# RMSNorm and Swish: transfers of 3, 5 and eight times 15 rows, computed in units of five rows

## The chip, the cores and the metric

The kernel runs on one core of a Trainium2 chip. The metric is the device time of one execution in microseconds (us); each number quoted is the median of several executions. The profile's span is about 2 us shorter than that time.

Engine names as in the profile: DVE is VectorE, ACT is ScalarE, POOL is GpSimd, SP is SyncE. ACTq and SPq are the sequencers of ACT and SP, which issue transfers. DMA stands for the core's 16 transfer engines, which carry the loads and stores between the off-chip memory (HBM) and the on-chip one (SBUF).

## The reference

```
x: 16 x 1024 x 512 float32, gamma: 512 ones, eps = 1e-5
rms    = sqrt(mean(x**2, axis=-1) + eps)
x_norm = x / rms * gamma
out    = x_norm * 1 / (1 + exp(-x_norm))        # Swish, or Silu
```

There are 16,384 rows of 512 numbers. Spread over 128 partitions that is 128 rows per partition, and below "a row" always means one row in each of the 128 partitions: 262,144 bytes. All data goes in once and out once, 2 x 33.55 MB.

## The kernel before

A list of sizes cuts the 128 rows into transfers. Loads are issued from SP, stores from ACT, into and out of one ring of 96 rows in SBUF. The computation goes in units ("chunks") of four rows, in four steps on three engines:

```python
sizes = [4, 4, 8] + [16] * 6 + [8, 8]      # rows of each load and each store
ring = 96
...
cn = 4                                     # rows of a unit
n_sq = 3                                   # of these, rows whose squares DVE sums
...
def sums(k):
    at = chunks[k]
    sq = squares_pool.tile([P, n_sq, D], fp32, name="sq")              # PSUM
    nc.scalar.activation(out=sq[:], in_=xb[:, at : at + n_sq, :], func=AF.Square, scale=inv_d**0.5)
    for j in range(n_sq, cn):              # the other rows: ACT squares and sums
        ...
        nc.scalar.activation(out=junk[:], in_=xb[:, at + j, :], func=AF.Square,
                             scale=inv_d**0.5, accum_out=ms[:, k, j : j + 1])
    nc.vector.tensor_reduce(out=ms[:, k, 0:n_sq], in_=sq[:], op=ALU.add, axis=mybir.AxisListType.X)
def root(k):                               # POOL: (ms + eps) ** -0.5
    ...
def norm(k):                               # DVE: row * rstd * gamma, one instruction per row
    for j in range(cn):
        row = xb[:, chunks[k] + j, :]
        nc.vector.scalar_tensor_tensor(out=row, in0=row, scalar=rstd[:, k, j : j + 1],
                                       in1=gamma_sb[:], op0=ALU.mult, op1=ALU.mult)
def swish(k):
    rows = xb[:, chunks[k] : chunks[k] + cn, :]
    nc.scalar.activation(out=rows, in_=rows, func=AF.Silu)
...
for k in range(K + 3):                     # software pipeline: sums k, norm k-1, swish k-2
    ...
    while stored < len(tiles) and ends[stored] <= k - 2:   # a transfer is stored when its last
        store(stored)                                      # unit has passed swish
    ...
```

A unit starts only when the whole load that holds it has landed (in the trace of this kernel the third load has landed at 12.97 us and the first square on it starts at 13.06; for the fourth it is 23.49 and 23.52), and a store is issued only when the last unit of its transfer has passed the Silu (the last Silu ends at 150.51, the last store is issued at 150.54).

## Time and profile before

The time is 162.77 us, median of 3 runs (162.57 to 162.83).

| | |
|---|---|
| span of the profile | 160.9 us |
| DVE busy, ACT busy | 139.1 us, 126.2 us |
| transfer time, (49.3% + 48.5%) of 160.9 us | 157.4 us |
| end of the last Silu | 150.5 us |

The page of the kernel before, from its first three parts: busy time of each engine; the busy share in 40 slices of 4 us, in tenths; bytes and packets; and the two queues (q1 loads, q10 stores) with packets, MB and the share of the time of all 16 transfer engines. The last line is the first one of the page's fourth part, the chain of waits that ended last.

```profile
span 160.9 us, 488 instructions
DVE 139.1 (86%) x162; ACT 126.2 (78%) x129; POOL 63.2 (39%) x70
DVE  0298977999999999999999999999999999999000
...
DMA  5999989899899999999999999899999999999994
...
DMA packets 3179, 67.14 MB, mean 417 GB/s; under 512 B 356, under 2 KB 356, under 8 KB 360
...
q1 hardware_dynamic: 1584, 33.56, 49.3%
q10 hardware_dynamic: 1592, 33.56, 48.5%
...
DVE 74%; DMA 13%; issue 2%; ACT 2%; SPq 1%; DVEq 1%
```

The chain says DVE, 74%. The queues say something else. The transfer engines are busy for 97.8% of the span, and their row of digits is full from the second slice to the last but one, while DVE's row begins late and ends three slices early. The chain follows the last instruction back, and the last compute instruction is the Silu that follows DVE; that the span goes on for 10 us after that Silu is a fact that the chain does not weigh.

The timeline of the kernel before at its end (start, duration, engine, line, instruction, in brackets the idle time before and what ended it):

```profile
143.18 5.38 DVE L108 SCALAR_TENSOR_TENSOR xb<-xb,rstd,gamma_sb 128x512 f32<-128x512 f32 x8
...
143.57 0.34 ACTq L76 DMA_DIRECT2D out_dram<-xb  x1
...
148.60 1.91 ACT L115 ACTIVATE xb<-xb 128x2048 f32<-128x2048 f32 x1 [0.74 <-DVE xb L108]
150.54 0.34 ACTq L76 DMA_DIRECT2D out_dram<-xb  x1
```

The last store, 8 rows, is issued at 150.54. The transfer engines are then still working on the store issued before it, at 143.57 (8 rows), which lands at 155.1; the one before that, issued at 134.94 (16 rows), has just landed, at 150.25. So there is no pause in front of the last store, and the last packets end at 159.6.

The groups of instructions of the kernel before that carry the DVE (busy time, mean of one in ns, then idle time before and what ended it):

```profile
L108 DVE SCALAR_TENSOR_TENSOR xb<-xb,rstd,gamma_sb 128x512 f32<-128x512 f32 x128 | 87.2, 743 | 0.0
L91 DVE TENSOR_REDUCE ms<-sq 128x3 f32<-128x1536 f32 x32 | 56.0, 1749 | 9.5 <-ACT sq L81 9.4
```

DVE waits for 9.4 us in all, all of it in the first 25 us, when data has not yet landed. After that it has no gap above 0.05 us between its reduces and products.

### The profile page before, as it was taken

To read this page: it belongs to the slowest core of one execution; us is meant where nothing else is said; L and a number is where in the kernel's file an instruction comes from. 1 tells how busy PE (TensorE), PEld (TensorE's weight loads), DVE (VectorE), ACT (ScalarE), POOL (GpSimd) and SP (SyncE) were. 2 spreads that over 40 slices of the span, in tenths; PEclk is the share of its full clock that TensorE was granted. 3 is DMA by queue.
4 is the path that set the end of the run, shared out by engine and by line. 5 is a ranking of instruction groups with operands and counts; after the bars stand their busy time and mean duration, and the time that the engine had idled before them with its cause. 6 is when DMAs were issued, how large, how long until landed. Compare 5 with 4: busy or idle time off the path is not lost.

```text
span 160.9 us, 488 instructions
## 1 busy us (share of the span) xinstructions
DVE 139.1 (86%) x162; ACT 126.2 (78%) x129; POOL 63.2 (39%) x70
## 2 busy tenths in 40 slices
DVE  0298977999999999999999999999999999999000
ACT  3557939988888888899888888888888899855400
POOL 1043442444444444444444444444444444441000
DMA  5999989899899999999999999899999999999994
GB/s 171 434 440 489 424 336 489 387 428 473 352 448 475 401 428 464 399 432 473 399 432 464 407 434 448 375 452 452 440 399 440 403 460 424 473 407 403 432 428 179
DMA packets 3179, 67.14 MB, mean 417 GB/s; under 512 B 356, under 2 KB 356, under 8 KB 360
## 3 DMA queue, kind: packets, MB, share of 16 engines
q1 hardware_dynamic: 1584, 33.56, 49.3%
q10 hardware_dynamic: 1592, 33.56, 48.5%
q14 instruction: 3, 0.02, 0.0%
HBM read 33.56 MB, written 33.55 MB: 417 GB/s over the span
## 4 chain that ended last, share of the span: by engine, by line
DVE 74%; DMA 13%; issue 2%; ACT 2%; SPq 1%; DVEq 1%
DVE xb L108 45%; DVE ms L91 29%; DMA xb<-in_x_dram 13%; ACT xb L115 1%; ACT sq L81 1%; SPq L73 1%; DVEq L182 1%; DVEq L108 0%
## 5 line engine op out<-in xcount | busy, mean ns | idle before, releaser
L108 DVE SCALAR_TENSOR_TENSOR xb<-xb,rstd,gamma_sb 128x512 f32<-128x512 f32 x128 | 87.2, 743 | 0.0
L115 ACT ACTIVATE xb<-xb 128x2048 f32<-128x2048 f32 x32 | 61.1, 1909 | 14.1 <-DVE xb L108 14.0
L91 DVE TENSOR_REDUCE ms<-sq 128x3 f32<-128x1536 f32 x32 | 56.0, 1749 | 9.5 <-ACT sq L81 9.4
L81 ACT ACTIVATE sq<-xb 128x1536 f32<-128x1536 f32 x32 | 46.0, 1439 | 7.8 <-DMA xb<-in_x_dram 7.8
L97 POOL TENSOR_SCALAR aeps<-ms 128x4 f32<-128x4 f32 x32 | 18.4, 575 | 79.1 <-DVE ms L91 79.1
L101 POOL TENSOR_TENSOR rstd<-aeps,neg_half 128x4 f32<-128x4 f32 x32 | 44.0, 1376 | 2.7
L87 ACT ACTIVATE junk_a<-xb 128x512 bf16<-128x512 f32 x32 | 19.6, 613 | 0.0
L87 ACT ACTIVATION_READ_ACCUMULATOR junk_a<-xb 128x1 f32 x32 | 6.0, 186 | 0.0
L121 ACT ACT_TABLE_LOAD x1 | 1.3, 1283 | 2.4 <-issue 2.4
L144 DVE STREAM_SHUFFLE gamma_sb<-gamma 128x512 f32<-128x512 f32 x1 | 0.7, 721 | 0.0
L118 POOL MEMSET gamma<- 128x512 f32 x1 | 0.5, 524 | 0.3 <-POOLq L168 0.3
L168 POOL MEMSET const-float32-0.0<- 128x1 f32 x1 | 0.1, 99 | 0.2 <-issue 0.2
L168 POOL MEMSET const-bfloat16-1.0<- 128x1 bf16 x1 | 0.1, 101 | 0.0
L168 POOL MEMSET const-uint8-127<- 128x1 uint8 x1 | 0.1, 101 | 0.0
L119 POOL MEMSET neg_half<- 128x4 f32 x1 | 0.1, 101 | 0.0
L168 POOL MEMSET const-float32-1.0<- 128x1 f32 x1 | 0.1, 98 | 0.0
L144 DVE LOAD_MASK_SELECT gamma_sb<-gamma x1 | 0.0, 14 | 0.0
## 6 DMA issues: line engine op xcount, KB each, us to landing
xb<-in_x_dram SPq DMA_DIRECT2D x6, 4096.0 KB, 42.5
out_dram<-xb ACTq DMA_DIRECT2D x6, 4096.0 KB, 29.8
xb<-in_x_dram SPq DMA_DIRECT2D x3, 2048.0 KB, 37.1
out_dram<-xb ACTq DMA_DIRECT2D x3, 2048.0 KB, 10.5
xb<-in_x_dram SPq DMA_DIRECT2D x2, 1024.0 KB, 5.9
out_dram<-xb ACTq DMA_DIRECT2D x2, 1024.0 KB, 20.0
gamma<-in_gamma_dram ACTq DMA_DIRECT2D x1, 8.0 KB
```

The source lines that it names most:

```text
L73: nc.sync.dma_start(out=buf(t), in_=dram(xf, t))
L81: nc.scalar.activation(out=sq[:], in_=xb[:, at : at + n_sq, :], func=AF.Square, scale=inv_d**0.5,)
L87: nc.scalar.activation(out=junk[:], in_=xb[:, at + j, :], func=AF.Square, scale=inv_d**0.5, accum_out=ms[:, k, j : j + 1],)
L91: nc.vector.tensor_reduce(out=ms[:, k, 0:n_sq], in_=sq[:], op=ALU.add, axis=mybir.AxisListType.X,)
L97: nc.gpsimd.tensor_scalar(out=aeps[:, k, :], in0=ms[:, k, :], scalar1=eps_f, scalar2=None, op0=ALU.add,)
L101: nc.gpsimd.tensor_tensor(out=rstd[:, k, :], in0=aeps[:, k, :], in1=neg_half[:], op=ALU.pow)
L108: nc.vector.scalar_tensor_tensor(out=row, in0=row, scalar=rstd[:, k, j : j + 1], in1=gamma_sb[:], op0=ALU.mult, op1=ALU.mult,)
L115: nc.scalar.activation(out=rows, in_=rows, func=AF.Silu)
L118: nc.gpsimd.memset(gamma4[:], 0.0)
L121: nc.scalar.preload_act_table_set("silu_and_others")
L144: nc.vector.stream_shuffle(gamma_sb[:], gamma4[:], [0] * 32)
L182: with _tile.TileContext(nc) as tc:
```

## The change

Its intent, as the diff shows it, is to take work off DVE, which the chain names. With units of five rows, DVE sums three and four rows in turn, 7 of 10 in place of 3 of 4, and ACT takes over the rest with one long Silu for five rows in place of four. The transfers are cut so that units of five fit: 3, 5 and eight times 15 rows, and the ring grows to 98 rows.

```diff
-    sizes = [4, 4, 8] + [16] * 6 + [8, 8]
-    ring = 96
+    sizes = [3, 5] + [15] * 8
+    ring = 98
     ahead = 32
-    cn = 4
-    n_sq = 3
+    cn = 5
+
+    n_sqs = (3, 4)
...
     def sums(k):
-        at = chunks[k]
-        sq = squares_pool.tile([P, n_sq, D], fp32, name="sq")
+        at, n = chunks[k]
+        n_sq = min(n, n_sqs[k % 2])
+        sq = squares_pool.tile([P, max(n_sqs), D], fp32, name="sq")
         nc.scalar.activation(
-            out=sq[:], in_=xb[:, at : at + n_sq, :], func=AF.Square,
+            out=sq[:, 0:n_sq, :], in_=xb[:, at : at + n_sq, :], func=AF.Square,
             scale=inv_d**0.5,
         )
-        for j in range(n_sq, cn):
+        for j in range(n_sq, n):
...
```

The rest of the diff carries the number of rows of each unit (n) through root, norm and swish, and rounds up where the number of units of a transfer is counted.

More of the change, by code (lines that the diff above doesn't have):

```diff
@@ L44 @@
         done += sz
-    chunks = [r for _, sz, at in tiles for r in range(at, at + sz, cn)]
+    chunks = [
+        (r, min(cn, at + sz - r))
+        for _, sz, at in tiles
+        for r in range(at, at + sz, cn)
+    ]
     K = len(chunks)
@@ L91, in sums @@
         nc.vector.tensor_reduce(
-            out=ms[:, k, 0:n_sq], in_=sq[:], op=ALU.add,
+            out=ms[:, k, 0:n_sq], in_=sq[:, 0:n_sq, :], op=ALU.add,
             axis=mybir.AxisListType.X,
@@ L96, in root @@
     def root(k):
+        n = chunks[k][1]
         nc.gpsimd.tensor_scalar(
-            out=aeps[:, k, :], in0=ms[:, k, :], scalar1=eps_f, scalar2=None,
+            out=aeps[:, k, 0:n], in0=ms[:, k, 0:n], scalar1=eps_f, scalar2=None,
             op0=ALU.add,
@@ L101, in root @@
         nc.gpsimd.tensor_tensor(
-            out=rstd[:, k, :], in0=aeps[:, k, :], in1=neg_half[:], op=ALU.pow
+            out=rstd[:, k, 0:n], in0=aeps[:, k, 0:n], in1=neg_half[:, 0:n], op=ALU.pow
         )
     def norm(k):
-        for j in range(cn):
-            row = xb[:, chunks[k] + j, :]
+        at, n = chunks[k]
+        for j in range(n):
+            row = xb[:, at + j, :]
             nc.vector.scalar_tensor_tensor(
@@ L113, in swish @@
     def swish(k):
-        rows = xb[:, chunks[k] : chunks[k] + cn, :]
+        at, n = chunks[k]
+        rows = xb[:, at : at + n, :]
         nc.scalar.activation(out=rows, in_=rows, func=AF.Silu)
@@ L132 @@
         for _, sz, _ in tiles:
-            e += sz // cn
+            e += -(-sz // cn)
             ends.append(e)
@@ L148 @@
                 swish(k - 2)
-                while loaded < len(tiles) and ends[loaded] <= k - 1 + ahead // cn + 2:
+                while loaded < len(tiles) and ends[loaded] <= k - 1 + -(-ahead // cn) + 2:
                     load(loaded)
```

## The prediction

> **What bounds it now.** Transfers. The page's DMA part: 67.14 MB; the two data queues take 49.3% + 48.5% = 97.8% of 16 engines' 160.9 us, 157.4 us of pure transfer (427 GB/s while busy[...]). The DMA row is 8 or 9 from slice 2 to slice 39: transfers never pause. The chain of waits names DVE (74%), because it follows the last Silu back, but after that Silu (148.60 + 1.91 = 150.5) the span has 10 us left, all of it queued stores. DVE is the second limit: from 25.0 us on it never waits (chain: 1.67 us reduce, 2.65 us for four row products, 4.32 per 4 rows), ending at 148.6.
>
> **What the change does.**
> - DVE: it reduces 7/10 of the rows instead of 3/4. The reduce is 1.67 us for 3 rows[...]. Ten rows: 1.67 + 2.20 + 10 x 0.662 = 10.5 us, 1.05 per row against 1.08: about 3.7 us less over 128 rows (estimate).
> - ACT: per ten rows two squares, three junk rows with accumulator reads, two five-row Silus: about 9.8 us (estimate from successive starts in the timeline: square 1.37, junk row 0.7, Silu 1.82). DVE stays the pacer.
> - Start: the third transfer is 15 rows, not 8. Today 16 rows have landed at 13.0 and 32 at 23.5 (0.66 us per row), so 23 rows land near 17.6. DVE waits there, then runs through: from 19.1, 24 reduces (46.4) + 125 products (82.8), ending at 148.4. The saving is spent: today DVE's unbroken run starts later (25.0), but with four chunks reduced. The last Silu has five rows (2.3 us): compute ends at 150.8 against 150.5.
> - End: the last store is 15 rows (3.93 MB, 9.1 us at full rate) instead of 8 (4.9 us). Loads and earlier stores (63.2 MB) need about 148 us of transfer from 1.75 us on, so the queues run dry near 150, before the last store (issued 150.9[...]). Then 152.4 + 9.1 + 0.4 landing + 0.9 closing = 162.8 us span, against 160.9.
> - Transfers: bytes and rate unchanged; the two loads that wait for ring rows stay some 8 us ahead of the compute.
>
> **On the critical path:** of DVE's 3.7 us nothing; transfers were already the limit. Of the coarser end about 2 us.
>
> **Prediction:** 164.8 us (time is 1.9 above the span), 8 in 10 between 163.3 and 166.3. Faster by over 2%: 0.02; within: 0.83; slower: 0.15.
>
> **What would show it.** Reduces of 1.75 (3 rows) and 2.28 us (4 rows), 13 each; DVE about 136 us busy. The third transfer's first square near 17.6. Last store issued near 150.9. DMA row: a dip of about 2 us just before the last store, absent today; total transfer time about 157 us. Last Silu's end to end of span 12 us, not 10.
>
> **What would make it wrong.** ACT and DVE interlock with alternating chunks (about 0.6 us of slack), so compute ends later: each us adds 1 us. Loads landing late for the last two tiles: some us. Stores still backlogged at the last issue: 161 to 163. Below 160 would need transfers beating 427 GB/s.

The cost of the fourth row in a reduce is the step from 1.67 to 2.20 us, and from 1.75 to 2.28 us under "What would show it" (scaled by rows from the 1.67 us of the trace, an estimate, the larger reduce would be 2.23 us, and ten rows again 10.5 us). The wait between the issue of the last store and its first packet is the step from 150.9 to 152.4. The sum itself came to 162.8 us of span (150.9, the wait, 9.1, 0.4 and 0.9), and with the 1.9 us between time and span to 164.7. Of its other terms, the trace of the kernel before has 0.33 us from the end of the last packet to the last landing and 0.91 us from there to the end of the span; the 9.1 us for 3.93 MB is an estimate, and at the 427 GB/s of that trace it would be 9.2.

## The result

The changed kernel takes 164.11 us, median of 4 runs (163.97 to 164.12); the kernel before, in the same rounds, 162.80 us (162.57 to 162.94). The ratio is 1.008, with a 95% interval of 1.0062 to 1.0097. A ratio here is the mean time of one kernel's runs over the mean of the other's of the same rounds, so it is not quite the ratio of the medians quoted. The change makes the kernel 0.8% slower, clear of the noise. The prediction was 164.8 us, range 163.3 to 166.3.

The page of the changed kernel, the same lines:

```profile
span 162.1 us, 460 instructions
DVE 135.9 (84%) x156; ACT 125.3 (77%) x127; POOL 55.2 (34%) x58
DVE  0375399999999999999999999999999999995000
...
DMA  5999999999999999999999999999999999997885
...
DMA packets 2891, 67.14 MB, mean 414 GB/s; under 512 B 324, under 2 KB 324, under 8 KB 584
...
q1 hardware_dynamic: 1440, 33.56, 48.8%
q10 hardware_dynamic: 1448, 33.56, 48.1%
...
DVE 76%; DMA 10%; issue 3%; ACT 2%; DVEq 1%; SPq 0%; ACTq 0%
```

DVE did get 3.2 us less to do (139.1 to 135.9). The transfers need what they needed: 96.9% of 162.1 us is 157.1 us. What is new stands at the right of the DMA row: its last four digits were 9, 9, 9, 4 and are 7, 8, 8, 5. The transfers now pause before the end.

The groups of the changed kernel, with the two forms of the reduce apart:

```profile
L117 DVE SCALAR_TENSOR_TENSOR xb<-xb,rstd,gamma_sb 128x512 f32<-128x512 f32 x128 | 86.7, 740 | 0.0
...
L98 DVE TENSOR_REDUCE ms<-sq 128x4 f32<-128x2048 f32 x13 | 29.6, 2280 | 1.1 <-ACT sq L88 1.1
...
L98 DVE TENSOR_REDUCE ms<-sq 128x3 f32<-128x1536 f32 x13 | 22.7, 1748 | 11.2 <-ACT sq L88 11.2
```

The idle time before the reduces rose from 9.5 to 12.3 us (1.1 + 11.2). So of the 3.2 us that DVE saves, 2.8 go into a longer wait at the start: the third load now brings 15 rows, and the first square on it starts at 17.45. The timeline of the changed kernel at its end:

```profile
141.49 6.70 DVE L117 SCALAR_TENSOR_TENSOR xb<-xb,rstd,gamma_sb 128x512 f32<-128x512 f32 x10
...
148.22 2.34 ACT L125 ACTIVATE xb<-xb 128x2560 f32<-128x2560 f32 x1 [0.98 <-DVE xb L117]
150.59 0.34 ACTq L82 DMA_DIRECT2D out_dram<-xb  x1
```

DVE ends at 148.19 in place of 148.56; the last Silu is 0.43 us longer, and the last store is issued at 150.59 in place of 150.54. Compute ends when it did. But this last store is now of 15 rows, and no whole transfer is queued in front of it: only the last packets of the store before are still moving. The windows view shows the pause: for a stretch of time, its length, busy time of DVE, ACT and POOL, the TensorE clock (of no interest here), and in the last two columns the busy share of the transfer engines and GB/s. First the kernel before, then the changed one. (A packet is booked where it starts, so short stretches can read a little over 1.00.)

```profile
149.00:151.00 2.00, 0.00 (x0) 1.51 (x1) 0.00 (x0) 1.00 1.00 426
151.00:156.00 5.00, 0.00 (x0) 0.00 (x0) 0.00 (x0) 1.00 0.99 426
```

```profile
149.00:151.00 2.00, 0.00 (x0) 1.56 (x1) 0.00 (x0) 1.00 0.07 31
151.00:156.00 5.00, 0.00 (x0) 0.00 (x0) 0.00 (x0) 1.00 0.92 393
```

Between 149 and 151 us packets for 426 GB/s start in the kernel before, for 31 GB/s in the changed kernel. Packets that started earlier still run there. Added up by the time in which they run (worked out from the packet records of the two traces), the 16 transfer engines of the changed kernel are idle for 2.0 us on average between 140 and 153 us, and all of them at once from 150.89 to 151.43; those of the kernel before are not idle there at all.

### The profile page after: what moved, and what is told of

It reads as the page before. It is cut to its first block, busy times and chain, and to the rows that moved or that the text cites. A ratio compares the mean times of both kernels' runs of the same rounds, so it can differ in the third digit from the quotient of the medians.

```text
span 162.1 us, 460 instructions
## 1 busy us (share of the span) xinstructions
DVE 135.9 (84%) x156; ACT 125.3 (77%) x127; POOL 55.2 (34%) x58
## 2 busy tenths in 40 slices
DMA packets 2891, 67.14 MB, mean 414 GB/s; under 512 B 324, under 2 KB 324, under 8 KB 584
## 4 chain that ended last, share of the span: by engine, by line
DVE 76%; DMA 10%; issue 3%; ACT 2%; DVEq 1%; SPq 0%; ACTq 0%
DVE xb L117 48%; DVE ms L98 28%; DMA xb<-in_x_dram 10%; ACT xb L125 1%; ACT sq L88 1%; SPq L79 0%; DVEq L192 0%; DVEq L117 0%; ACTq L88 0%
## 5 line engine op out<-in xcount | busy, mean ns | idle before, releaser
L125 ACT ACTIVATE xb<-xb 128x2560 f32<-128x2560 f32 (+1 forms) x26 | 59.9, 2303 | 13.1 <-DVE xb L117 13.0
L98 DVE TENSOR_REDUCE ms<-sq 128x3 f32<-128x1536 f32 (+1 forms) x26 | 52.4, 2014 | 12.3 <-ACT sq L88 12.3
L88 ACT ACTIVATE sq<-xb 128x1536 f32<-128x1536 f32 (+1 forms) x26 | 42.9, 1652 | 9.8 <-DMA xb<-in_x_dram 9.8
L105 POOL TENSOR_SCALAR aeps<-ms 128x5 f32<-128x5 f32 (+1 forms) x26 | 15.1, 581 | 86.1 <-DVE ms L98 56.4
L109 POOL TENSOR_TENSOR rstd<-aeps,neg_half 128x5 f32<-128x5 f32 (+1 forms) x26 | 39.3, 1512 | 2.2
L94 ACT ACTIVATE junk_a<-xb 128x512 bf16<-128x512 f32 x37 | 22.7, 613 | 0.0
L94 ACT ACTIVATION_READ_ACCUMULATOR junk_a<-xb 128x1 f32 x37 | 6.9, 186 | 0.0
```

The lines of the kernel that those rows point to most:

```text
L88: nc.scalar.activation(out=sq[:, 0:n_sq, :], in_=xb[:, at : at + n_sq, :], func=AF.Square, scale=inv_d**0.5,)
L98: nc.vector.tensor_reduce(out=ms[:, k, 0:n_sq], in_=sq[:, 0:n_sq, :], op=ALU.add, axis=mybir.AxisListType.X,)
L105: nc.gpsimd.tensor_scalar(out=aeps[:, k, 0:n], in0=ms[:, k, 0:n], scalar1=eps_f, scalar2=None, op0=ALU.add,)
L109: nc.gpsimd.tensor_tensor(out=rstd[:, k, 0:n], in0=aeps[:, k, 0:n], in1=neg_half[:, 0:n], op=ALU.pow)
```

## The experiments

Theory A, from the prediction: the transfers set the time of both kernels. Compute only has to keep the queues from running dry. The changed kernel loses time because its last store is coarse and compute ends no earlier, so that the queues run dry before that store can start.

Rival B: the units of five or the 15-row transfers cost by themselves, through the pacing of DVE and ACT or through ragged packets.

Rival C: DVE sets the time, as the chain of waits suggests, and the changed kernel spoils its DVE saving somewhere else.

Eight kernels ran, in two groups of four; each group shares its runs of the kernel before (162.73 us in the first, 162.75 us in the second, 11 runs each). The two groups ran on different chips, so each run is compared with the kernel before of its own group first.

### e1: the last store in three pieces

The last 15-row tile is loaded as one but stored as three stores of 5 rows, each after its own Silu.

```diff
-    def store(t):
-        nc.scalar.dma_start(out=dram(of, t), in_=buf(t))
+    def store(t, a, b):
+        nc.scalar.dma_start(out=dram(of, t)[:, a:b, :], in_=buf(t)[:, a:b, :])
...
+        # pieces: (units done, tile, first row, end row); one for each tile, three for the last
-            while stored < len(tiles) and ends[stored] <= k - 2:
-                store(stored)
+            while stored < len(pieces) and pieces[stored][0] <= k - 2:
+                store(*pieces[stored][1:])
```

> The changed kernel, with only the store of the last 15-row tile cut into three stores of 5 rows, each issued after its Silu. Theory A (transfers limit; the changed kernel loses the pause before its coarse last store): compute ends where it does now (last Silu about 150.5), but the first two pieces are queued early enough that the transfer engines never pause; span about 160.4, time about 162.3, that is at or just under the kernel before, 1.1% under the changed kernel. Rival B (the changed kernel is paced by its DVE and ACT, or by ragged 30 KB transfers): the last Silu ends at the same time, so time stays near 164.1.

Measured: 163.06 us (162.46 to 163.40, 6 runs), ratio to the kernel before 1.0014 (0.9992 to 1.0035), against 1.008 for the whole change; the two intervals do not overlap. The pause is gone: the windows view of this run for the same two stretches shows

```profile
149.00:151.00 2.00, 0.71 (x2) 1.26 (x1) 0.00 (x0) 1.00 0.90 384
151.00:156.00 5.00, 0.00 (x0) 1.07 (x1) 0.00 (x0) 1.00 1.00 426
```

The time came back although compute was even later in the profiled run: its last Silu ended at 152.1, not 150.6, because one small POOL instruction took 3.25 us and DVE waited 1.4 us for it (more on this at the end). A later end of compute together with an earlier end of the program speaks against B and C. The median lies 0.8 us above the expected 162.3, and the reason is not shown: in the profile kept the transfer engines do not pause (0.90 and 1.00 busy in the two stretches). The six runs spread over 0.9 us; the eleven of the kernel before in this group spread over 1.0 us.

### e2: the kernel before with a coarse end

```diff
-    sizes = [4, 4, 8] + [16] * 6 + [8, 8]
+    sizes = [4, 4, 8] + [16] * 7
```

> The kernel before, units of four rows, with only its end made coarse: the last two tiles of 8 rows become one of 16. Theory A: DVE and ACT as before (last Silu ends about 150.5), the queues run dry about 149, last store starts about 151.4 and takes 9.7 us; span about 162.4, time about 164.3, as slow as the changed kernel. Rival B (units of five or 15-row transfers are what costs): no more than 0.3 us over the kernel before, 162.8 to 163.1.

Measured: 164.83 us (164.77 to 166.22, 6 runs), ratio 1.0154 (1.0121 to 1.0186). Four runs lie at 164.8, two at 166.0 and 166.2; the profile that was kept is of one of the four, so what costs the other two more is open. Its windows:

```profile
148.00:149.00 1.00, 0.79 (x2) 0.26 (x2) 0.00 (x0) 1.00 0.31 131
149.00:151.00 2.00, 0.00 (x0) 1.73 (x1) 0.00 (x0) 1.00 0.00 0
```

With units of four rows, with DVE's old work and with nothing altered but the last two tiles, the same pause appears and the kernel is at least as slow as after the whole change. The coarse end is sufficient.

### e3 and e4: the same delay in both kernels

In one unit in the middle, the reduce of three rows is issued three times with the same result.

```diff
-        nc.vector.tensor_reduce(
-            ...
-        )
+        for _ in range(3 if k == 16 else 1):      # e3, kernel before; k == 12 in e4, changed kernel
+            nc.vector.tensor_reduce(
+                ...
+            )
```

> The kernel before, with DVE's reduce of unit 16 done three times (same result): 3.3 us more DVE work on the chain that the profile names as the longest. Theory A: last Silu ends 3.3 us later (about 153.9), its store is then still behind 8 rows of queued stores or just meets their end (they end at 154.7), so the time stays within 0.4 us of the kernel before. Rival C (DVE sets the time, as the chain with its 74% suggests): 3.3 us more, 166.1.

> The changed kernel with the same extra work, DVE's 3-row reduce of unit 12 done three times. Theory A: here no queue is left to hide it, so the whole 3.3 us appear: last Silu about 153.9, time about 167.4. If the changed kernel had slack like the kernel before: 164.1 to 164.5. Rival C expects 167.4 too; it is the pair with the run of the kernel before that tells them apart.

Measured: e3 takes 163.64 us (163.46 to 163.88, 6 runs), ratio 1.0055 (1.0038 to 1.0071); e4 takes 167.41 us (167.34 to 168.92, 6 runs), ratio 1.0305 (1.0272 to 1.0338).

In the profile of e3 the last store is issued at 154.32, 3.8 us later than without the delay, and the time rises by 0.9 us. In that of e4 it is issued at 154.10, 3.5 us later, and the median is 3.3 us above the 164.11 of the changed kernel. (The two were not measured in the same rounds, so the difference is good to some tenths; the spans, 165.6 and 162.1, give 3.5.) The kernel before has some 3 us of slack behind its queue (an estimate: 3.8 less 0.9); the changed kernel has none (3.5 less 3.3). e3 missed its expectation of "within 0.4 us" by half a microsecond: compute ended 3.8 us later and not 3.3, and the queue seems to have just run out (from 151 to 156 us the busy share of the transfer engines is 0.87, against 0.99 in the kernel before). The last stores of e3 and of e4 in their timelines:

```profile
154.32 0.34 ACTq L76 DMA_DIRECT2D out_dram<-xb  x1
```

```profile
154.10 0.34 ACTq L82 DMA_DIRECT2D out_dram<-xb  x1
```

Rival C needs the full delay in both kernels. It falls with e3.

### e5: the changed kernel with a finer start

```diff
-    sizes = [3, 5] + [15] * 8
+    sizes = [3, 5, 5, 10] + [15] * 7
```

> The changed kernel with only its start made finer: transfers of 3, 5, 5, 10 and seven of 15 rows; the last store stays one of 15 rows. Theory A: DVE waits less at the start (one unit of five rows is reduced before row 13 lands), so compute ends about 4 us earlier (last Silu about 146), the last store is queued before the queues run dry, the pause is gone and the transfers alone set the time: span 160.4 to 160.9, time 162.3 to 162.8. Rival B (15-row transfers or units of five cost by themselves at the end of the kernel): 164.1. Rival C (DVE sets the time): 160, four less than the changed kernel.

Measured: 162.72 us (162.50 to 162.89, 6 runs), ratio 0.9995 (0.9982 to 1.0007). The last store is still one of 15 rows, the units are still of five and the ring still has 98 rows. Only the wait at the start is shorter: DVE's idle time before the reduces is 7.9 us in place of 12.3, and the last store is issued at 146.31 in place of 150.59. Four microseconds earlier, it finds the queue still working:

```profile
145.00:148.00 3.00, 0.00 (x0) 1.28 (x1) 0.00 (x0) 1.00 0.95 410
148.00:149.00 1.00, 0.00 (x0) 0.00 (x0) 0.00 (x0) 1.00 0.85 369
149.00:151.00 2.00, 0.00 (x0) 0.00 (x0) 0.00 (x0) 1.00 1.07 461
```

The pause is gone, and the time is that of the kernel before, not 4 us less. Both halves matter. B falls, because units of five and coarse transfers, the last one included, cost nothing here once the queue does not run dry (ratio 0.9995). And compute that ends 4 us earlier wins nothing beyond closing the pause.

### e6: the transfers of the change with units of four rows

```diff
-    cn = 5
+    cn = 4
-    n_sqs = (3, 4)
+    n_sqs = (3, 3)
```

> The transfers and the ring of the changed kernel with units of four rows and three rows reduced by DVE, as in the kernel before (15 rows make units of 4, 4, 4 and 3). It tells what the units of five contribute. Theory A: DVE has 34 reduces in place of 26 (about 6 us more work), which here has nothing to hide behind: last Silu about 155.5, last store starts 156.3, time about 168.5 to 170. Rival (DVE work does not matter at all, because the transfers limit both): 164.1.

Measured: 169.08 us (168.99 to 169.13, 4 runs), ratio 1.0386 (1.0373 to 1.0399). DVE is busy for 143.0 us, the last store is issued at 155.31, and the queues stand still for more than 5 us; the windows view has

```profile
150.00:156.00 6.00, 3.70 (x6) 3.39 (x2) 1.13 (x1) 1.00 0.00 0
```

So the saving on DVE is not worthless inside the change: with these transfers it is worth about 5 us (169.08 against 164.11, not measured in the same rounds). The cut of the transfers costs 6.3 us, and the units of five give most of that back. Some of the 6.3 is due to ragged units (15 rows make 4, 4, 4 and 3, which is 35 units and 35 reduces; the expectation counted 34), which this run does not separate.

### e7: the kernel before with half of DVE's products left out

```diff
     def norm(k):
-        for j in range(cn):
+        for j in range(2):
```

Half of the rows are not normalised (relative error 0.027). Its output is wrong, which doesn't matter for the time.

> The kernel before with two of every four row products left out (wrong result on purpose): 42 us less DVE work. Theory A: the transfers still need their 157.4 us from 1.7 us on, so span 160.0 to 160.6 and time 162.0 to 162.5, at most 0.5% less, though DVE is idle a third of the time. Rival C (DVE sets the time, 74% of the chain): ACT would pace at about 3.9 us per unit, 12 us earlier, time about 151.

Measured: 162.34 us (162.30 to 162.36, 4 runs), ratio 0.9972 (0.9959 to 0.9985). The page of this run:

```profile
span 160.5 us, 423 instructions
DVE 99.3 (62%) x98; ACT 123.4 (77%) x129; POOL 63.1 (39%) x70
...
DMA  4999989799899999999999999999999999999994
```

DVE has 40 us less to do, the last store is issued at 145.74, almost 5 us earlier, and the time falls by 0.4 us. This run also measures what these transfers take when compute ends 5 us earlier: about 162.3 us. ACT still has its whole work here, 123.4 us.

### e8: fine start and split store together

This is e5 with the three pieces of e1, the version with most slack.

> Fine start and the last store in three pieces together, with units of five: the version with most slack. Theory A: nothing more to win once no pause is left, so the same as either of the two alone and as the kernel before within 0.3%: 162.2 to 162.7. If it comes clearly below 162, the transfers had a reserve that theory A denies.

Measured: 162.75 us (162.47 to 162.97, 6 runs), ratio 0.9996 (0.9984 to 1.0008). As expected there is nothing more to win. I found no correct version that beats both kernels by more than the noise, and e7 shows why: the kernel before is within 0.3% of what its transfers took there.

| kernel | time, us | last store issued, us | DMA share, 149 to 151 us |
|---|---|---|---|
| before | 162.75 | 150.54 | 1.00 |
| the change | 164.11 | 150.59 | 0.07 |
| e1 the change, last store in pieces | 163.06 | 152.10 (5 rows) | 0.90 |
| e2 before, coarse end | 164.83 | 150.76 | 0.00 |
| e5 the change, fine start | 162.72 | 146.31 | 1.07 |
| e6 the transfers of the change alone | 169.08 | 155.31 | 0.58, then 0.00 |
| e7 before, DVE light | 162.34 | 145.74 | 0.96 |
| e8 the change, fine start, last store in pieces | 162.75 | 146.16 (5 rows) | 0.95 |

The runs with the delay, e3 and e4, are left out here: their last stores come 3.5 us later or more, after this stretch.

## Why the prediction was right

**What bounds the kernel: right.** The prediction set the transfers, 157.4 us of pure work, above the chain's 74% for DVE. e7 takes 40 us from DVE and wins 0.4; e3 adds 3.5 us of DVE work and loses 0.9. The rate while busy is 427 GB/s in the kernel before (67.14 MB in 157.4 us) and the same in the changed kernel (in 157.1 us).

**DVE's saving: right.** Reduces of 1.748 and 2.280 us, 13 each (predicted 1.75 and 2.28), DVE 135.9 us busy (predicted about 136). The estimate "about 3.7 us less" was too high: it is 3.2 us (139.1 to 135.9). The fourth row costs 0.53 us (2.280 less 1.748).

**The start takes the saving: right.** The third load's first square starts at 17.45 (predicted 17.6), DVE begins its reduce at 18.93 (19.1) and ends at 148.19 (148.4). e5, which alters only the start, returns 4 us to compute.

**The coarse end costs the pause: right, and e2 shows it alone.** The last store was issued at 150.59 (predicted 150.9), when only two packets of 30 KB had started since 149 (31 GB/s over the 2 us). The engines' mean idle time of 2.0 us is the predicted dip of about 2 us. The span grew by 1.2 us only, mainly because the changed kernel gains something at the very end: there its 16 transfer engines finish almost together (0.06 us of mean idle time from 153 us to the end of the last packet), where those of the kernel before finish unevenly (0.8 us).

**One term was mis-sized: the wait before the last store's first packet.** The prediction forecast 1.9 us more span (162.8 against 160.9), the profiles show 1.2. Its sum holds 1.5 us for this wait (152.4 less 150.9), the author's estimate, which was not worked out from a trace. In the trace of the changed kernel the first packet of the last store starts at 151.43, 0.84 us after its issue. With 0.84 in place of 1.5 the prediction's sum would be 162.1 us of span, which is what was measured; that it fits so exactly is partly luck, since the other small errors cancel (issue 0.3 us earlier, the transfer 9.3 us and not 9.1, 1.4 us and not 1.3 from the last packet to the end).

**One side remark was too easy: "the two loads that wait for ring rows stay some 8 us ahead".** The last load landed at 125.2, and the first square on its rows started at 126.17. It was 1 us ahead, not 8, and the load before it 3 us (landed at 107.0, first square at 110.18). This cost nothing here, since ACT waited for loads three times only, the last until 17.45. Whether a slower store would have stalled the kernel no run shows.

**A sign that was described too boldly:** the dip of 2 us is hardly to be seen in the page's row of digits (7, 8, 8, 5), because slices are 4 us and the packets of the last store go in step, 1.1 us each, and are booked where they start. The windows view shows it at once.

## What to carry to other kernels

Where the queues are busy for nearly all of the span, as here for 98%, ask of a change to compute first whether the queues will run dry, and look at the end: in these runs the pause went away when the last store was small (e1) or was queued while others were still in front of it (e5). A chain of waits that ends in compute names the engine behind the last instruction, which need not be the limit (here it gave DVE 74%, and the 40 us that e7 took from DVE won 0.4); the cheap test is to add and to take work on that engine and see whether the time follows. In this kernel coarse transfers at the two ends were paid with idle time that used up the saving in the middle, and finer ones at the start (e5) did as well as finer ones at the end (e1).

## What else the traces show

- POOL's small addition took longer where it started during DVE's first row product of a unit. In the kernel before it took 0.23 us in the first unit, where no product runs, and 0.58 to 0.59 us in the 31 others, where it started 0.24 us after the start of that product and ended 0.09 us after its end. In the changed kernel it was 0.24 us once and 0.59 to 0.60 us 25 times, and these 25 ended 0.09 to 0.10 us after the product. In e1 one addition, started at 141.74, lasted 3.25 us, to 144.99, which is 0.10 us after the end of the whole run of five products (144.89). The timeline of e1:

```profile
141.48 3.41 DVE L117 SCALAR_TENSOR_TENSOR xb<-xb,rstd,gamma_sb 128x512 f32<-128x512 f32 x5
141.74 3.25 POOL L105 TENSOR_SCALAR aeps<-ms 128x5 f32<-128x5 f32 x1 [3.30 <-ACT xb L125]
```

- What links these times no run shows. Among the additions listed of nine profiles (all but e4) the next longest took 0.67 us, in e6. Whether such a wait makes the longest runs of e1, e2 and e4 is not shown either: no trace was kept of any of them.
- The packet records have a median of 1.213 us for a packet of 32 KB (kernel before) and 1.138 us for one of 30 KB (changed kernel), both 27.0 GB/s.
- In the changed kernel, from the start of the issuing instruction on ACT to the first packet of the last store, on idle queues, it was 0.84 us; from the end of that instruction (0.34 us long) it was 0.50 us.
